# Two kinds of gate columns transposed by one product per block of tokens, the second kind at column 32 of a padded tile

## The chip, the cores and the metric

The kernel runs on one core of a Trainium2 chip. Its metric is the device time of one execution in microseconds (us), the median of several runs. A core has TensorE (PE: matrix products and transposes into PSUM), VectorE (DVE), ScalarE (ACT), GpSimd (POOL) and SyncE (SP), which here issues most of the transfers; all of them work on their own queues and wait for one another by semaphores. SBUF is the working memory of 128 partitions, and PSUM holds the results of products, in banks of 512 float32 per partition.

## The reference

One layer of a streaming encoder, for a prompt of 2048 tokens and a sample of 64 tokens with a state. A normalised and modulated input goes through one projection `w_in`, whose columns are a pooling input `u`, `q`, `k`, `v`, `o` and eight gate columns per token:

```
u, q, k, v, o, gates = jnp.split(proj, cuts, -1)
gates = gates.astype(jnp.float32) + b_gate.astype(jnp.float32)
ig = gates[..., :N_HEADS]                       # 4 input gates
lf = jax.nn.log_sigmoid(gates[..., N_HEADS:])   # 4 forget gates
...
b = jnp.cumsum(lf, -1)
dmat = b[..., :, None] - b[..., None, :] + ig[..., None, :]
```

The gates drive a matrix memory with four heads, computed in chunks. Its output and the pooling output go through `w_out`, then a gated feed-forward part with a causal convolution of width 3, and a last normalisation. All values are float32.

## The kernel before

The tokens are worked on in four attention groups of 512 tokens, the last of which has the 64 sample tokens as well (576 in all), and after all four in three feed-forward groups of 704 tokens. Activations lie transposed (features on partitions, tokens along the free dimension), and weights are streamed from HBM: SP loads them, ScalarE copies a rounded high part (line 366), VectorE subtracts it to get a low part (line 369), and each product is made of three passes over these parts. From group 1 on most attention weights come back already split (`hl_kept`, loaded by line 355).

In each attention group, `proj_v` makes the values and the gate columns first: here the activations `h` are the stationary operand, so the result has tokens on partitions, in up to five blocks (four of 128 tokens, in the last group one more of 64). The half `hv` = 1 of the weights has 264 columns: 256 of `v` and the eight gate columns. `out` copies those eight to the tile `gt` on VectorE (line 1094) and the `v` columns to `va` on ScalarE (line 1095), from the same PSUM tile. `gate_rows` then turns the gate columns into rows of tokens on four partitions (lines 1117 and 1118 transpose, 1120 adds the bias of the input gates on ScalarE, 1121 that of the forget gates on VectorE), and goes on with the log-sigmoid (lines 1125 to 1132), two scans along the tokens (1135, 1143), differences of these (1147 to 1163), a transpose back (1172) and the small tiles CL and GL that the heads use. Four heads follow (`proj_qko` with products at line 423, `lstm` at lines 1218 to 1299), then pooling and the output projection.

`gate_rows` and most other side work are generators in lists (`bg`); the loops over products call `tick`, which lets the first generator of a list run to its next `yield`, so their pieces are spread among the large products. Among the side work are the modulation sums on VectorE (`ada`, lines 201 and 203, weights loaded by line 188) and weight sums for the feed-forward part (`up_sums`, lines 843 to 868).

For the start of group 0, with its `proj_v`, and for the whole feed-forward part, the order on PE, ACT, DVE and POOL is the order of the program text (`manual_schedule`). For the rest of the attention part, and for SP's transfers throughout, a planner orders each queue by program order and its own estimate of when things are ready; it also places the tiles in memory and sets the semaphores. Small PSUM tiles are taken in turn from two pools of two banks each:

```
turn = {"mm": [large] * 4, "m2": [small, small, third, third]}
```

`m2_ps()` gives the next of the "m2" banks, `mm_ps()` one of the four large ones. `sm` is an SBUF pool with two buffers for a tile such as `gt`; the pools `a1` and `a2`, with the tiles of the attention part, are laid out behind it. `ident` is the 128 x 128 identity, and `RV` holds the two gate biases as columns.

Of the kernel before, what the change touches and what calls it, by code (L numbers as in the profile page):

```python
# [9 lines left out]
F32 = mybir.dt.float32  # L10
F32R = mybir.dt.float32r
AF = mybir.ActivationFunctionType
# [4 lines left out]
P = 128  # L17
# [42 lines left out]
def tile_layer(ctx: ExitStack, tc: tile.TileContext, xT, vecs, cst, rst, rowv, w_mod, w_ada, w_qkou, w_v, w_pool,  # L60
               w_out, w_up, w_down, st_C, st_pool, yT, o_pool, o_C, o_m, o_conv):
    nc = tc.nc
    act, dve, pool, pe = nc.scalar, nc.vector, nc.gpsimd, nc.tensor
# [9 lines left out]
    def bank(nm, shape=(P, 512)):  # L73
        q = turn[nm]
        q.append(q.pop(0))
        return q[-1].tile(list(shape), F32, tag="bank", name=nm)
# [3 lines left out]
    def mm_ps():  # L80
        return bank("mm")

    def m2_ps():
        return bank("m2")
# [7 lines left out]
    sm = actx.enter_context(tc.tile_pool(name="sm", bufs=2))  # L92

    def scr():
        return sp.tile([P, TMAX], F32, tag="scr", name="scr")
# [4 lines left out]
    def tick(i=0):  # L100
        q = bg[i]
        while q:
            try:
                next(q[0])
                return
            except StopIteration:
                q.pop(0)
# [25 lines left out]
    ident = cp.tile([P, P], F32, tag="ident", name="ident")  # L133
    nc.sync.dma_start(out=ident, in_=cst[:, C_ID:C_ID + P])
    RV = cp.tile([4, 3], F32, tag="RV", name="RV")
# [197 lines left out]
    class Unit:  # L333

        state = 0
        w = raw = None
# [494 lines left out]
    if True:  # L831
# [237 lines left out]
        def proj_v(o, h, cols):  # L1069
            nt = len(o.chunks)  # L1070
            va = a1.tile([P, 5, NH, 129], F32, tag="va", name="va")
            pool.memset(va[:, :, :, 128:129], 1.0)
            gt = sm.tile([P, 5, 8], F32, tag="gt", name="gt")

            def part(hv, kh, tis, ps, W):
                cols = VC[hv]
                for ti in tis:
                    lo, n, s = o.chunks[ti]
                    for k4 in range(4):
                        U = W.at(k4 // 2)  # L1080
                        for pi, (a, b) in enumerate(PASSES):
                            pe.matmul(ps[ti][:n, :cols], h[4 * kh + k4][:, b, lo:lo + n],  # L1082
                                      U[:, a, k4 % 2 * cols:(k4 % 2 + 1) * cols],
                                      start=(kh == 0 and k4 == 0 and pi == 0),
                                      stop=(kh == 1 and k4 == 3 and pi == 2))
                    if hv == 1 or ti % 2:
                        tick(0)
                tick(1)

            def out(hv, tis, ps):  # L1090
                for ti in tis:
                    n = o.chunks[ti][1]
                    if hv == 1:
                        dve.tensor_copy(gt[:n, ti, :], ps[ti][:n, 256:264])
                    act.activation(va[:n, ti, 2 * hv:2 * hv + 2, 0:128],
                                   ps[ti][:n, :256].rearrange("p (h v) -> p h v", v=128), AF.Copy)

            for hv in (1, 0):
                if o.g == 0:
                    out(hv, range(4), ps_v[1 - hv])  # L1100
                else:
                    ps = [mm_ps() if ti < 4 else m2_ps() for ti in range(nt)]
                    for kh in range(2):
                        part(hv, kh, range(nt), ps, Row())
                    out(hv, range(nt), ps)
                if hv == 1:
                    bg[0].append(gate_rows(o, gt, cols))
            return va

        def gate_rows(o, gt, cols):  # L1110
            T = o.T
            ir, z = scr(), scr()
            for (a, b, n, s) in o.tsegs:
                pi_, pf_ = m2_ps(), m2_ps()
                for ti in range(a, b):
                    c0 = (ti - a) * n
                    pe.transpose(pi_[:4, c0:c0 + n], gt[:n, ti, 0:4], ident[:n, :n])
                    pe.transpose(pf_[:4, c0:c0 + n], gt[:n, ti, 4:8], ident[:n, :n])
                w = (b - a) * n
                act.activation(ir[:4, a * P:a * P + w], pi_[:4, :w], AF.Identity, bias=RV[:, 0:1])  # L1120
                dve.tensor_scalar(out=z[:4, a * P:a * P + w], in0=pf_[:4, :w], scalar1=RV[:, 1:2], scalar2=None,
                                  op0=ALU.add)
            yield
            e = scr()
            dve.scalar_tensor_tensor(out=e[:4, :T], in0=z[:4, :T], scalar=-1.0, in1=z[:4, :T],
                                     op0=ALU.mult, op1=ALU.max)
            act.activation(e[:4, :T], e[:4, :T], AF.Exp, scale=-1.0)
            yield
            act.activation(e[:4, :T], e[:4, :T], AF.Ln, bias=1.0)
            yield  # L1130
            lf = z
            dve.scalar_tensor_tensor(out=lf[:4, :T], in0=z[:4, :T], scalar=0.0, in1=e[:4, :T],
                                     op0=ALU.min, op1=ALU.subtract)
            b_ = scr()
            dve.tensor_tensor_scan(out=b_[:4, :T], data0=RST[:, :T], data1=lf[:4, :T], initial=0.0,
                                   op0=ALU.mult, op1=ALU.add)
            mo = [1, GT + 2]
            for (a, b, s) in o.segs:
                w = b - a
                m0 = mo[s]  # L1140
                if s == 0 and o.g > 0:
                    dve.tensor_copy(M[:, 0:1], M[:, GT:GT + 1])
                dve.tensor_tensor_scan(out=M[:, m0:m0 + w], data0=lf[:4, a:b], data1=ir[:4, a:b],
                                       initial=M[:, m0 - 1:m0], op0=ALU.add, op1=ALU.max)
            yield
            cc = e
            dve.tensor_tensor(out=cc[:4, :T], in0=ir[:4, :T], in1=b_[:4, :T], op=ALU.subtract)
            act.activation(R4[0:4, :T], cc[:4, :T], AF.Copy)
            r = ir
            for (a, b, n, s) in o.tsegs:  # L1150
                lo, w, m0 = a * P, (b - a) * n, mo[s]
                dve.tensor_tensor(out=r[:4, lo:lo + w], in0=b_[:4, lo:lo + w], in1=M[:, m0:m0 + w], op=ALU.subtract)
                act.activation(R4[64:68, lo:lo + w], M[:, m0:m0 + w], AF.Copy, scale=-2.0)

                def v3(ap):
                    return ap.rearrange("p (t c) -> p t c", c=n)
                mp = v3(M[:, m0 - 1:m0 - 1 + w])[:, :, 0:1].broadcast_to([4, b - a, n])
                dve.tensor_tensor(out=v3(R4[32:36, lo:lo + w]), in0=v3(r[:4, lo:lo + w]), in1=mp, op=ALU.add)
                rl = v3(r[:4, lo:lo + w])[:, :, n - 1:n].broadcast_to([4, b - a, n])
                dve.tensor_tensor(out=v3(R4[96:100, lo:lo + w]), in0=v3(cc[:4, lo:lo + w]), in1=rl, op=ALU.add)  # L1160
            yield
            act.activation(RHL[0:4, :T], r[:4, :T], AF.Copy)
            dve.tensor_tensor(out=RHL[32:36, :T], in0=r[:4, :T], in1=RHL[0:4, :T].bitcast(F32), op=ALU.subtract)
            for _ in range(8):
                yield

            CL = sm.tile([P, 5, 4, 4], F32, tag="CL", name="CL")
            GL = sm.tile([P, 20], F32, tag="GL", name="GL")
            for (a, b, n, s) in o.tsegs:
                pt = m2_ps()  # L1170
                for ti in range(a, b):
                    pe.transpose(pt[:n, (ti - a) * P:(ti - a + 1) * P], R4[:, ti * P:ti * P + n], ident)
                for qn in range(4):
                    src = pt[:n, :(b - a) * P].rearrange("p (t c) -> p t c", c=P)[:, :, 32 * qn:32 * qn + 4]
                    if qn == 0:
                        dve.tensor_copy(CL[:n, a:b, qn, :], src)
                    else:
                        act.activation(CL[:n, a:b, qn, :], src, AF.Exp)
            for _ in range(4):
                yield  # L1180
            pb = m2_ps()
            for (a, b, n, s) in o.tsegs:
                sel = C[:n, (C_L127 if s == 0 else C_L63):][:, :P]
                pe.matmul(pb[:, 4 * a:4 * b], sel, CL[:n, a:b, 1, :], start=True, stop=True)
            dve.tensor_copy(GL[:, :4 * len(o.chunks)], pb[:, :4 * len(o.chunks)])
            cols += [CL, GL]
            yield
# [179 lines left out]
        for o in groups:  # L1367
# [45 lines left out]
            for gi in U_ORDER:  # L1413
                ps = proj(o, h)
                pg = poolmix(o, gi, ps, mix[gi])
# [301 lines left out]
    for o in fgroups:  # L1717
        Bo = B[o.g]
        for pi, (f0, f1_) in enumerate(PARTS):
# [82 lines left out]
            for secs in [(c,) for c in ENDS] if ends else (both,):  # L1802
                sums = [(ssum, 0)]
                for n in range(NE, KD):
                    ps = [mm_ps() for _ in secs]
# [92 lines left out]
```

## Time and profile before

| what | value |
|---|---|
| median of three runs | 2223.43 us (2221.27 to 2223.73) |
| the profiled execution, its own time | 2221.81 us |
| its span, first to last instruction | 2220.0 us |
| mean granted clock of TensorE | 0.997 |
| transpose of input-gate columns, line 1117 | 17 products |
| transpose of forget-gate columns, line 1118 | 17 products |
| copy into `gt`, line 1094 | 17 instructions |
| gate transposes at, groups 0 to 3 | 53.5, 228.6, 411.8 and 603.0 us |

Times within the profile are microseconds from the start of its span, or nanoseconds for single instructions where said. In the rows below, `m<-ident,gt 128*4 128x128` is a product that writes a small PSUM tile, with a stationary operand of 128 rows and 4 columns and a moving one of 128 x 128; `x17` is a count; in brackets stands the idle time of the engine before the instruction and what ended it. LDWEIGHTS (PEld) is the load of the stationary operand, which can overlap with products that are under way. The chain of waits follows the end of the execution back through what released each step; a duration there is the part of the instruction that lies on the chain.

### The profile page before, as it was taken

To read this page: it belongs to the slowest core of one execution; us is meant where nothing else is said; L and a number is where in the kernel's file an instruction comes from. 1 tells how busy PE (TensorE), PEld (TensorE's weight loads), DVE (VectorE), ACT (ScalarE), POOL (GpSimd) and SP (SyncE) were. 2 spreads that over 40 slices of the span, in tenths; PEclk is the share of its full clock that TensorE was granted. 3 is DMA by queue.
4 is the path that set the end of the run, shared out by engine and by line. 5 is a ranking of instruction groups with operands and counts; after the bars stand their busy time and mean duration, and the time that the engine had idled before them with its cause. 6 is when DMAs were issued, how large, how long until landed. Compare 5 with 4: busy or idle time off the path is not lost.

```text
span 2220.0 us, 38121 instructions
## 1 busy us (share of the span) xinstructions
PE 2193.5 (99%) x13798; PEld 2079.9 (94%) x13798; DVE 1567.5 (71%) x2901; ACT 1005.1 (45%) x1992; POOL 200.5 (9%) x480
## 2 busy tenths in 40 slices
PE   8999999999999999999999999999999999999998
PEld 7888888888899999999999999999999999999998
DVE  5877659577765768687858677677767685757474
ACT  3553334234343446464636444545445353445254
POOL 0010000001000101010000210000001210101012
PEclk9999999999999999999999999999999999999999
DMA  9968987997898685657656865556458554353442
GB/s 364 331 240 269 337 275 237 319 315 244 289 321 272 215 304 183 224 168 262 209 175 219 280 228 199 185 193 203 152 163 281 187 196 158 110 180 120 145 152 81
DMA packets 279358, 498.58 MB, mean 225 GB/s; under 512 B 25177, under 2 KB 105433, under 8 KB 279169
## 3 DMA queue, kind: packets, MB, share of 16 engines
q1 hardware_dynamic: 267392, 468.05, 63.3%
q10 hardware_dynamic: 11776, 28.09, 3.4%
q8 instruction: 109, 1.79, 0.3%
q14 instruction: 81, 0.66, 0.1%
HBM read 385.29 MB, written 110.75 MB: 223 GB/s over the span
## 4 chain that ended last, share of the span: by engine, by line
PE 91%; DMA 3%; DVE 3%; ACT 1%; issue 1%; SPq 0%; POOL 0%; POOLq 0%; ACTq 0%; DVEq 0%
PE mm L1487 37%; PE mm L423 24%; PE mm L1749 21%; PE mm L1082 3%; DMA wt<-wsum 1%; PE m L1263 1%; PE m L1264 1%; PE mm L1013 1%; PE m L1241 1%; PE m L1252 1%; PE m L1344 1%; PE p L1013 0%; PE m L1231 0%; PE m L1294 0%; DVE wt L369 0%
## 5 line engine op out<-in xcount | busy, mean ns | idle before, releaser
L1487 PE MATMUL mm<-hx,wt 128*128 128x352 f32 x5544 | 885.9, 321 | 4.2 <-DVE ea L1539 2.6
L1487 PEld LDWEIGHTS mm<-hx,wt 128*128 128x128 f32 x5544 | 879.1, 188 | 6.5 <-ACT wt L366 3.9
L1749 PE MATMUL mm<-av,wt 128*128 128x352 f32 (+2 forms) x3168 | 509.3, 321 | 0.5 <-DVE av L1610 0.3
L1749 PEld LDWEIGHTS mm<-av,wt 128*128 128x128 f32 x3168 | 502.6, 188 | 3.4 <-DVE av L1610 0.9
L423 PE MATMUL mm<-hl,wt 128*128 128x512 f32 (+2 forms) x1920 | 397.4, 358 | 3.9 <-DMA wt<-hl_kept 2.7
L369 DVE TENSOR_TENSOR wt<-raw,wt 128x512 fp32r<-128x512 f32 (+3 forms) x494 | 306.9, 637 | 90.6 <-ACT wt L366 85.8
L366 ACT ACTIVATE wt<-raw 128x512 fp32r<-128x512 f32 (+3 forms) x494 | 271.8, 570 | 212.7 <-PE mm L1749 83.5
L423 PEld LDWEIGHTS mm<-hl,wt 128*128 128x128 f32 x1920 | 312.3, 188 | 52.5 <-issue 6.5
L1764 DVE SCALAR_TENSOR_TENSOR x<-mm,MOD,x 128x352 f32<-128x352 f32 (+4 forms) x224 | 106.5, 526 | 115.5 <-PE mm L1749 115.4
L423 PE MATMUL mm<-mx,wt 128*128 128x512 f32 (+1 forms) x960 | 186.6, 353 | 0.0
L423 PEld LDWEIGHTS mm<-mx,wt 128*128 128x128 f32 x960 | 158.7, 188 | 25.2 <-ACT mx L1346 1.2
L1475 DVE SCALAR_TENSOR_TENSOR tg<-eg,V,tg 128x704 f32<-128x704 f32 (+1 forms) x132 | 125.7, 952 | 50.6 <-ACT tg L1470 48.3
L369 DVE TENSOR_TENSOR wt<-wt 128x512 fp32r<-128x512 f32 x176 | 121.9, 693 | 52.1 <-ACT wt L366 51.8
L366 ACT ACTIVATE wt<-wt 128x512 fp32r<-128x512 f32 x176 | 110.1, 626 | 81.4 <-DMA wt<-wsum 70.9
L1475 DVE SCALAR_TENSOR_TENSOR ta<-ea,V,ta 128x704 f32<-128x704 f32 (+1 forms) x132 | 125.6, 952 | 8.3 <-ACT ta L1470 5.9
L1610 DVE TENSOR_TENSOR av<-tg,av 128x704 fp32r<-128x704 f32 (+4 forms) x112 | 62.1, 588 | 45.1 <-ACT av L1602 44.8
L1581 ACT ACTIVATE tg<-tg 128x704 f32<-128x704 f32 (+1 forms) x66 | 52.4, 794 | 81.6 <-DVE tg L1475 76.0
L1535 ACT ACTIVATE u<-mm 128x352 f32<-128x352 f32 x66 | 30.5, 462 | 121.5 <-PE mm L1487 84.0
L1495 DVE TENSOR_TENSOR eg<-mm,u 128x352 f32<-128x352 f32 x154 | 70.1, 467 | 20.8 <-ACT u L1550 11.1
L203 DVE SCALAR_TENSOR_TENSOR acc<-raw,CA,acc 128x512 f32<-128x512 f32 x84 | 60.4, 744 | 31.7 <-DMA raw<-w_ada 31.7
L1082 PE MATMUL mm<-wt,hl 128*128 128x256 f32 (+1 forms) x576 | 70.9, 282 | 0.0
L1082 PEld LDWEIGHTS mm<-wt,hl 128*128 128x128 f32 x576 | 69.2, 188 | 1.0 <-issue 0.6
(293 smaller groups left out, 1950.9 us busy)
## 6 DMA issues: line engine op xcount, KB each, us to landing
wt<-hl_kept SPq DMA_DIRECT2D x108, 512.0 KB, 5.8
raw<-w_up SPq DMA_DIRECT2D x198, 256.0 KB, 3.8
wt<-wsum SPq DMA_DIRECT2D x176, 256.0 KB, 4.2
wt<-wsplit SPq DMA_DIRECT2D x88, 512.0 KB, 4.1
raw<-w_down SPq DMA_DIRECT2D x96, 256.0 KB, 2.8
w<-w_up SPq DMA_DIRECT2D x88, 256.0 KB, 5.7
wsum<-w SPq DMA_DIRECT2D x44, 512.0 KB, 6.4
wsplit<-wt SPq DMA_DIRECT2D x44, 512.0 KB, 4.6
```

The source lines that it names most:

```text
L203: dve.scalar_tensor_tensor(out=acc[s], in0=w, scalar=CA[:, k, s:s + 1], in1=acc[s], op0=ALU.mult, op1=ALU.add)
L366: act.activation(u.w[:, 0, :u.n], u.raw[:, :u.n], AF.Copy)
L369: dve.tensor_tensor(out=u.w[:, 1, :u.n], in0=u.raw[:, :u.n], in1=u.w[:, 0, :u.n].bitcast(F32), op=ALU.subtract)
L423: pe.matmul(ps[bi][:, :hi - lo], U[:, a, k % 4 * P:(k % 4 + 1) * P], mv[k][:, b, lo:hi], start=(at == 0 and pi == 0), stop=(k == order[-1] ...
L1082: pe.matmul(ps[ti][:n, :cols], h[4 * kh + k4][:, b, lo:lo + n], U[:, a, k4 % 2 * cols:(k4 % 2 + 1) * cols], start=(kh == 0 and k4 == 0 and ...
L1475: dve.scalar_tensor_tensor(out=t[:, :E], in0=ext[:, j:j + E], scalar=wc(j, f), in1=t[:, :E], op0=ALU.mult, op1=ALU.add)
L1487: pe.matmul(ps[:, :FH], U[:, a, kc * P:(kc + 1) * P], Bo.at(nm, kc, b), start=(first and kc == 0 and pi == 0), stop=(kc == 3 and pi == 2), ...
L1495: dve.tensor_tensor(out=ext[:, d:d + b - a], in0=ps[:, a:b], in1=u[:, a:b], op=ALU.add)
L1581: act.activation(self.tg[:, :E], self.tg[:, :E], AF.Silu)
L1610: dve.tensor_tensor(out=cut(1), in0=self.of_tg(cut(0), a, b), in1=cut(0).bitcast(F32), op=ALU.subtract)
L1749: pe.matmul(ps[i][:, :hi - lo], U[:, a, k % 4 * P:(k % 4 + 1) * P], av[k](b, lo, hi), start=(k == 0 and (a, b) == PASSES[0]), stop=(k == n ...
L1764: dve.scalar_tensor_tensor(out=x3[n][:, a:b], in0=ps[i][:, a - lo:b - lo], scalar=gt2(n, s), in1=x3[n][:, a:b], op0=ALU.mult, op1=ALU.add)
```

## The change

The tile `gt` grows from 8 to 36 columns per block and is cleared on GpSimd. The four input-gate columns stay at columns 0 to 3, the four forget-gate columns go to columns 32 to 35. One transpose of 36 columns for each block takes the place of two of 4 columns, into one PSUM tile `pg` in the place of `pi_` and `pf_`; ScalarE reads its rows 0 to 3 and VectorE its rows 32 to 35.

```
-            gt = sm.tile([P, 5, 8], F32, tag="gt", name="gt")
+            gt = sm.tile([P, 5, 36], F32, tag="gt", name="gt")
+            pool.memset(gt, 0.0)
...
                     if hv == 1:
-                        dve.tensor_copy(gt[:n, ti, :], ps[ti][:n, 256:264])
+                        dve.tensor_copy(gt[:n, ti, :].rearrange("p (a b) -> p a b", b=4)[:, 0:9:8, :],
+                                        ps[ti][:n, 256:264].rearrange("p (a b) -> p a b", b=4))
...
             for (a, b, n, s) in o.tsegs:
-                pi_, pf_ = m2_ps(), m2_ps()
+                pg = m2_ps()
                 for ti in range(a, b):
                     c0 = (ti - a) * n
-                    pe.transpose(pi_[:4, c0:c0 + n], gt[:n, ti, 0:4], ident[:n, :n])
-                    pe.transpose(pf_[:4, c0:c0 + n], gt[:n, ti, 4:8], ident[:n, :n])
+                    pe.transpose(pg[:36, c0:c0 + n], gt[:n, ti, :], ident[:n, :n])
                 w = (b - a) * n
-                act.activation(ir[:4, a * P:a * P + w], pi_[:4, :w], AF.Identity, bias=RV[:, 0:1])
-                dve.tensor_scalar(out=z[:4, a * P:a * P + w], in0=pf_[:4, :w], scalar1=RV[:, 1:2], scalar2=None,
+                act.activation(ir[:4, a * P:a * P + w], pg[:4, :w], AF.Identity, bias=RV[:, 0:1])
+                dve.tensor_scalar(out=z[:4, a * P:a * P + w], in0=pg[32:36, :w], scalar1=RV[:, 1:2], scalar2=None,
                                   op0=ALU.add)
```

## The prediction

> **What bounds the kernel now.** I read the page first, for the engine that fills the span and the chain that ended last.
>
> ```profile
> span 2220.0 us, 38121 instructions
> PE 2193.5 (99%) x13798; PEld 2079.9 (94%) x13798; DVE 1567.5 (71%) x2901; ACT 1005.1 (45%) x1992; POOL 200.5 (9%) x480
> PE 91%; DMA 3%; DVE 3%; ACT 1%; issue 1%; SPq 0%; POOL 0%; POOLq 0%; ACTq 0%; DVEq 0%
> ```
>
> TensorE is busy for 2193.5 of 2220.0 us and carries 91% of the chain, so a product taken off its queue is worth its place in that queue, as long as no other engine or transfer is late next. The change works on the gate columns, so the second view was that of the two lines that transpose them.
>
> ```profile
> L1117 PEld LDWEIGHTS m<-ident,gt x17: 78/84/85, 53.2 to 604.0; 128*4 128x4 f32 x16, 64*4 64x4 f32 x1
> L1117 PE MATMUL m<-ident,gt x17: 214/272/273, 53.5 to 604.0; 128*4 128x128 f32 x16, 64*4 64x64 f32 x1
> L1118 PE MATMUL m<-ident,gt x17: 215/273/273, 53.6 to 604.1; 128*4 128x128 f32 x16, 64*4 64x64 f32 x1
> ```
>
> There are 34 of them: 16 blocks of 128 tokens and one of 64, twice. Their 272 ns are durations, not places in the queue. For the places I took the timeline of TensorE in group 1 and the chain of waits in group 3:
>
> ```profile
> 228.57 0.27 PE L1117 MATMUL m<-ident,gt 128*4 128x128 f32 x1
> 228.68 0.27 PE L1118 MATMUL m<-ident,gt 128*4 128x128 f32 x1
> ...
> 229.33 0.27 PE L1118 MATMUL m<-ident,gt 128*4 128x128 f32 x1
> ...
> 604.07 0.14 PE m L1117
> 604.21 0.06 PE m L1118
> ```
>
> From 228.57 to 229.33 seven steps pass, 0.109 us each. The 64-token product costs 0.06 us on the chain. Third, who stops TensorE in the attention stage, and how full the transfers are around the gate work (the columns are busy times of PE, PEld, DVE, ACT and POOL, then granted clock, DMA share, GB/s):
>
> ```profile
> PE mm L423 <- DMA wt<-hl_kept: 2.7, 2, 2.4
> PE m L1263 <- DVE st L1257: 1.7, 1, 1.7
> PE mm L423 <- DVE wt L369: 0.8, 1, 0.8
> PE mm L423 <- ACT wt L366: 0.5, 1, 0.5
> 225.00:290.00 65.00, 65.00 (x384) 55.18 (x383) 43.85 (x98) 23.76 (x63) 2.54 (x3) 1.00 0.97 330
> 405.00:470.00 65.00, 62.33 (x371) 52.33 (x370) 44.10 (x90) 21.22 (x50) 2.46 (x2) 0.97 0.91 310
> 600.00:690.00 90.00, 88.28 (x676) 83.42 (x674) 57.87 (x144) 36.31 (x105) 4.20 (x5) 1.00 0.93 311
> ```
>
> After the gate transposes of group 1 TensorE never stops (65.00 of 65.00 us); in group 2 it loses 2.67 us and in group 3 1.72 us, with the DMA engines at 0.91 to 0.97. In those stretches time saved on TensorE can be lost to a transfer.
>
> **The change part by part: products removed.** The seventeen products of L1118 go: 16 x 0.109 + 0.06 = 1.80 us of TensorE's queue, 0.44 us in each of groups 0 to 2 and 0.50 us in group 3. The seventeen that stay load 36 columns in place of 4. Bounds for that are transposes of full 128-column tiles:
>
> ```profile
> L1172 PEld LDWEIGHTS m<-ident,R x17: 110/141/143, 70.4 to 628.0; 128*128 128x128 f32 x16, 128*64 128x64 f32 x1
> 70.75 0.44 PE m L1172 x4
> 95.44 0.59 PE m L1231 x4
> ```
>
> Even with 128 columns, whose load takes 141 ns where 4 take 84, a transpose holds the chain for 0.44 / 4 = 0.110 us, at worst 0.148 (L1231). A load of 36 columns lies between, nearer to 4, and is hidden under the product before it: I take 0, with a bound of 17 x (0.148 - 0.109) = 0.66 us. By the Trainium skill, "TensorE: Matmul & The Clock Gate", section "LDWEIGHTS (loading the stationary operand)", a load costs its columns over 1.2, in ns, which speaks against the padding: 32 more columns are an estimated 27 ns for each of the 17, 0.45 us that the sum would lose if loads were not hidden. The trace doesn't bear it out in that form, since 124 more columns cost 57 ns of load and about 1 ns of pitch.
>
> **Products removed: what is late next.** Group 0's order is written by hand and its chain runs through the gates:
>
> ```profile
> 54.43 0.68 ACT L1120 ACTIVATE scr<-m,RV 4x512 f32<-4x512 f32 x1 [1.01 <-PE m L1117]
> 54.54 0.74 DVE L1121 TENSOR_SCALAR scr<-m,RV 4x512 f32<-4x512 f32 x1 [2.59 <-PE m L1118]
> 55.12 1.28 ACT L1127 ACT_TABLE_LOAD   x1
> 55.31 0.68 DVE L1125 SCALAR_TENSOR_TENSOR scr<-scr 4x512 f32<-4x512 f32 x1
> 56.42 0.63 ACT L1127 ACTIVATE scr<-scr 4x512 f32<-4x512 f32 x1
> ...
> 62.05 0.65 DVE L1147 TENSOR_TENSOR scr<-scr 4x512 f32<-4x512 f32 x1
> 62.64 0.67 DVE L369 TENSOR_TENSOR wt<-raw,wt 128x512 fp32r<-128x512 f32 x1
> 63.36 2.80 PE L423 MATMUL mm<-hl,wt 128*128 128x512 f32 x11 [0.77 <-DVE wt L369]
> ```
>
> TensorE waits here at 63.36 us for VectorE, which is behind the gate arithmetic. So group 0 gains not its 0.44 us, but what the gate chain gains. ScalarE starts when the last of the i-transposes is done, three products earlier than now: 54.43 - 0.33 = 54.10. VectorE must now read the tile that ScalarE reads. A row of the waits shows that these two are put one behind the other when they read one PSUM tile:
>
> ```profile
> ACT va L1095 <- DVE gt L1094: 33.6, 13, 9.6
> ```
>
> So I count this as an added wait: z (L1121) starts at 54.10 + 0.68 + 0.02 = 54.80 and not at 54.54, and L1125 ends at 54.80 + 0.74 + 0.03 + 0.68 = 56.25. The exponential needs that and its table (54.79 + 1.28 = 56.07), so it starts at about 56.30 in place of 56.42. Group 0 gains 0.12 us; without the added wait, the table's end decides and it gains 0.33. Queued behind z on VectorE are L1125 and the low parts of the weights (L369), and on these TensorE waits. By the Trainium skill, "PSUM — Partial Sum Buffer", section "PSUM bank collisions raise a hardware error", two engines must be kept apart only on one bank and one quadrant of 32 partitions; rows 0 to 3 and 32 to 35 are different quadrants, so by that rule no wait would be needed, and the sum would be 0.21 us better. No run here shows such a pair yet.
>
> In group 2 the first stop of any size after the transposes is a transfer:
>
> ```profile
> 432.88 0.67 DVE acc L203
> 433.55 0.14 SPq L188
> ...
> 433.79 7.19 DMA wt<-hl_kept
> ...
> 441.12 0.94 PE mm L423 x3
> ```
>
> The weights that TensorE waits for 2.42 us were issued behind VectorE's modulation sums, which wait for transfers themselves; the gate step is not what held them. I take group 2's 0.44 us as lost in this wait (bound: all of it kept). Group 1 has no stop behind it and keeps 0.44. In group 3 the transfers ahead of the stop at 676.8 us follow TensorE's own progress, so I let it keep 0.50.
>
> **The two engines and GpSimd.** The copies into the padded tile have the same 8 values in two runs of 4; the row bounds a change at a few ns, and ScalarE's copy behind each is not on the chain. The clearing of the padded tile is new, 128 x 180 values, four times:
>
> ```profile
> L1072 POOL MEMSET va<- x4: 133/134/134, 14.2 to 519.2; 128x20 f32 x4
> L1052 POOL MEMSET R<- 128x576 f32 x1 | 0.6, 577 | 0.0
> L1094 DVE COPY gt<-mm x16: 154/164/167, 49.6 to 600.7; 128x8 f32<-128x8 f32 x16
> ```
>
> It lies between 0.13 and 0.58 us, about 0.25. It follows the clearing of va, which is at 14.2 us for a copy at 49.6, and at 519.2 for one near 600. GpSimd is 9% busy. The cover is some 35 us at the least: nothing. Without that cover it would cost its 0.25 us per group.
>
> **Placement.** The padded tile is 720 bytes per partition and not 160, in two buffers, so the tiles that are laid out after it move by 1.1 KB or so. The rows show the like only as the two pitches of a transpose, 0.110 and 0.148; 68 transposes at L1231 between these are 68 x 0.038 = 2.6 us either way. Nothing in the profile ties the pitch to an address, so I take 0.
>
> **Sum.** 0.12 + 0.44 + 0 + 0.50 = 1.06 us, bounds 0 and 1.80. The profiled execution took 2221.81 us, 1.81 over its span and 1.62 under the median of 2223.43. So it would become about 2220.7, and the median 2222.4: 0.05% faster. About 0.2%, or 4.4 us, can be told from no change.
>
> **The rivals.** *A, the planner's order gets worse: slower.* In groups 1 to 3 the order of each queue comes from a planner that starts from its own estimate of times; the change moves z behind ScalarE, takes products out and moves a bank of PSUM on for all later small tiles. Place: VectorE in front of the sums of L203. Their reads free the buffers for the next w_ada loads, and behind these on SP stands wt<-hl_kept, as at 433.55 us. Price: a load of weights one place later costs the measured 2.4 us. It decides from the point where the new waits exceed 4.4 + 1.06 = 5.5 us, that is from three of them. One in each of the three stretches gives 2222.4 + 7.2 = 2229.6. For it: DMA shares of 0.91 to 0.97 leave no room to catch up. Against it: in group 1 TensorE doesn't stop even at 0.97, and VectorE has idle time where z stands (before L1121 in group 0, 2.59 us).
>
> *B, the order gets better: faster.* If the new order happens to remove the two stops of groups 2 and 3 as well, the gain is 2.7 + 1.7 + 1.80 = 6.2 us: 2217.2. For it: both stops are small accidents of order between transfers. Against it: it needs both, and nothing in the change aims at them.
>
> *C, a transpose is worth its duration: faster.* At 272 ns each, the seventeen would be 17 x 0.272 = 4.6 us: 2218.8. The Trainium skill, "TensorE: Matmul & The Clock Gate", "Part 4: PE-mode transpose", gives about 275 ns in one kernel's context, as the duration row here has it. The steps of 0.109 us between starts speak against it.
>
> *D, no gain left: no change.* The wider load and the stops take all of it: 2223.4.
>
> **How the numbers follow.** My forecast of 2222.4 gets 0.42 and D 0.08, both within 0.2%: 0.50. A gets 0.30, since the scheduled stretches are full of transfers and a chance order has more ways to cost than to gain. B gets 0.17 and C 0.03: 0.20 for faster. The range goes down to 2216.5, just past B, and up to 2230.0, just past A's three waits; about 0.05 is left below and 0.15 above. The likeliest case alone lies from 2221.6 (all 1.80 us kept) to 2223.4.
>
> **What would show it.** Right: 17 products with a 128x36 load at about 0.11 us of the queue, 17 instructions fewer for PE; in group 0 ScalarE's first gate step earlier by 0.3 us against TensorE, and VectorE's z directly behind ScalarE's end; waits of TensorE between 110 and 760 us close to 4.4 us in all. A would show as further rows "PE mm L423 <- DMA wt<-hl_kept" or stops on VectorE in those stretches, B as both rows gone. If the difference lies in the feed-forward stage, behind 800 us, or in the pitch of products that the change doesn't touch, the prediction is wrong in its reasons whatever the time.

## The result

| what | before | after |
|---|---|---|
| median of 12 runs each, alternating | 2223.31 us (2220.58 to 2226.88) | 2226.64 us (2224.34 to 2231.53) |
| ratio, 95% interval | | 1.0021 [1.0014, 1.0029] |
| profiled execution, its own time | 2221.81 us | 2228.43 us |
| longest stop of TensorE in group 0 behind the gates | 0.77 us | 2.84 us |
| mean granted clock | 0.997 | 0.995 |

The change makes the kernel slower, by 0.21%, about 4.7 us (3.1 to 6.4); the ratio is taken over all the runs, and the two medians by themselves lie 3.3 us apart. The change does what it says: the page of the changed kernel has 17 products fewer, and the load of 36 columns takes 98 ns.

```profile
span 2226.6 us, 38087 instructions
PE 2198.3 (99%) x13781; PEld 2080.3 (93%) x13781; DVE 1567.9 (70%) x2901; ACT 1003.9 (45%) x1992; POOL 202.6 (9%) x484
PE 92%; DMA 2%; DVE 2%; ACT 1%; issue 1%; POOL 0%; SPq 0%; ACTq 0%; POOLq 0%; DVEq 0%
```

```profile
L1119 PEld LDWEIGHTS m<-ident,gt x17: 93/98/99, 54.9 to 611.3; 128*36 128x36 f32 x16, 64*36 64x36 f32 x1
L1119 PE MATMUL m<-ident,gt x17: 229/272/273, 55.1 to 611.3; 128*36 128x128 f32 x16, 64*36 64x64 f32 x1
```

TensorE is busy 4.8 us longer with fewer products. So the same products must have run slower somewhere, and the place is found by laying the starts of the same large products beside each other, after minus before (products into `mm` with 256 moving columns or more, by their count in the trace):

| product number | 96 | 108 | 132 | 156 | 720 | 840 | 1440 | 1620 | 2160 | 2340 | end |
|---|---|---|---|---|---|---|---|---|---|---|---|
| us later | 1.64 | 1.23 | 1.55 | 6.32 | 7.21 | 6.60 | 6.78 | 6.41 | 7.64 | 7.22 | 6.62 |

Numbers 96 to 108 enclose the gate transposes of group 0. The loss, 4.77 us, comes between 132 and 156, just behind them. The next three pairs (720 and 840, 1440 and 1620, 2160 and 2340) enclose the gate transposes of groups 1 to 3, and each gains. The 1.64 us ahead of the gates arise where both kernels do the same; in the profiles of the runs below, the delay that a kernel brings from its first 33 us lay between -0.8 and +2.2.

Here are ScalarE and VectorE in the changed kernel's timeline for that place (start, busy time, engine, line, operation; in brackets the idle time before it and what ended it):

```profile
55.74 0.68 ACT L1121 ACTIVATE scr<-m,RV 4x512 f32<-4x512 f32 x1 [0.83 <-PE m L1119]
56.46 0.74 DVE L1122 TENSOR_SCALAR scr<-m,RV 4x512 f32<-4x512 f32 x1 [3.16 <-ACT scr L1121]
...
57.95 0.63 ACT L1128 ACTIVATE scr<-scr 4x512 f32<-4x512 f32 x1 [0.22 <-DVE scr L1126]
...
59.88 0.60 ACT L1192 ACTIVATE q<-mm 128x512 f32<-128x512 f32 x1 [1.30 <-PE mm L423]
60.49 1.28 ACT L1130 ACT_TABLE_LOAD   x1
...
61.79 0.63 ACT L1130 ACTIVATE scr<-scr 4x512 f32<-4x512 f32 x1
62.72 0.63 ACT L366 ACTIVATE wt<-raw 128x512 fp32r<-128x512 f32 x1 [0.30 <-DMA raw<-w_qkou]
...
65.65 0.63 ACT L1154 ACTIVATE R<-M 4x512 f32<-4x512 f32 x1 [2.30 <-DVE M L1144]
66.30 0.63 ACT L366 ACTIVATE wt<-raw 128x512 fp32r<-128x512 f32 x1
```

And ScalarE in the kernel before:

```profile
57.07 1.28 ACT L1129 ACT_TABLE_LOAD   x1
58.36 0.63 ACT L1129 ACTIVATE scr<-scr 4x512 f32<-4x512 f32 x1
58.90 0.57 ACT L1191 ACTIVATE q<-mm 128x512 f32<-128x512 f32 x1
61.17 0.63 ACT L366 ACTIVATE wt<-raw 128x512 fp32r<-128x512 f32 x1 [1.70 <-DMA raw<-w_qkou]
62.22 0.63 ACT L1153 ACTIVATE R<-M 4x512 f32<-4x512 f32 x1 [0.42 <-DVE M L1143]
```

Before, ScalarE loads the table and takes the logarithm (L1129), and then copies q (L1191). After, the copy of q (L1192) stands ahead of the logarithm (L1130): ScalarE waits 1.30 us for TensorE's q product, and only then loads the table and takes the logarithm, which starts at 61.79 in place of 58.36 (1.23 us of that is the delay that this execution has at product 108). The scans follow it on VectorE. ScalarE's copy of the scan (L1154) now waits 2.30 us, and the high part of the next weights (L366, 66.30) is queued behind that copy. These are TensorE's rows for the same 31 products, the first from the changed kernel's timeline, the second from that of the kernel before:

```profile
66.98 10.09 PE L423 MATMUL mm<-hl,wt 128*128 128x512 f32 x31 [2.84 <-ACT wt L366]
```

```profile
63.36 7.38 PE L423 MATMUL mm<-hl,wt 128*128 128x512 f32 x31 [0.77 <-DVE wt L369]
```

TensorE stops 2.84 us, and then its 31 products take 10.09 us where the same 31 took 7.38 before. The windows say why (PE, PEld, DVE, ACT and POOL busy, then granted clock, DMA share, GB/s), first after:

```profile
67.00:70.00 3.00, 3.00 (x7) 2.42 (x8) 2.90 (x5) 2.01 (x4) 0.00 (x0) 0.50 1.05 406
70.00:73.00 3.00, 3.00 (x8) 2.29 (x8) 2.97 (x8) 0.91 (x2) 0.00 (x0) 0.52 1.05 407
73.00:76.00 3.00, 3.00 (x15) 2.45 (x14) 3.00 (x5) 0.97 (x1) 0.00 (x0) 1.00 1.06 403
```

then before:

```profile
67.00:70.00 3.00, 3.00 (x15) 2.46 (x14) 3.00 (x7) 1.37 (x2) 0.00 (x0) 1.00 1.05 391
```

For some six microseconds behind the stop the granted clock is about one half, and TensorE makes 7 or 8 products in three microseconds in place of 15. PE shows as busy all that time. The sum for the place: stops 0.81 + 2.84 after against 0.49 + 0.77 before, 2.39 us; slower products 10.09 - 7.38 = 2.71 us; together 5.10, beside the measured 5.09 between products 108 and 156 (6.32 - 1.23). The first of the two stops lies ahead of product 132, so 4.77 us come behind it.

So the theory to be tested: z has to wait for ScalarE on the shared PSUM tile; the planner, which counts this, orders ScalarE's queue in group 0 in another way; a stop of over two microseconds follows, and it costs as much again in clock. The rivals: the padded, moved and cleared tile costs the time by itself; or fewer products, by moving everything after them, change the order.

### The profile page after: what moved, and what is told of

The parts are those of the page before. It is cut to its first block, busy times and chain, and to the rows that moved or that the text cites. A ratio compares the mean times of both kernels' runs of the same rounds, so it can differ in the third digit from the quotient of the medians.

```text
span 2226.6 us, 38087 instructions
## 1 busy us (share of the span) xinstructions
PE 2198.3 (99%) x13781; PEld 2080.3 (93%) x13781; DVE 1567.9 (70%) x2901; ACT 1003.9 (45%) x1992; POOL 202.6 (9%) x484
## 3 DMA queue, kind: packets, MB, share of 16 engines
q8 instruction: 109, 1.79, 0.3%
## 4 chain that ended last, share of the span: by engine, by line
PE 92%; DMA 2%; DVE 2%; ACT 1%; issue 1%; POOL 0%; SPq 0%; ACTq 0%; POOLq 0%; DVEq 0%
PE mm L1488 37%; PE mm L423 24%; PE mm L1750 21%; PE mm L1083 3%; DMA raw<-w_down 1%; PE m L1253 1%; PE m L1242 1%; PE mm L1013 1%; PE m L1264 1%; PE m L1265 1%; PE m L1345 1%; PE p L1013 0%; PE m L1232 0%; PE m L1295 0%; DVE wt L369 0%
## 5 line engine op out<-in xcount | busy, mean ns | idle before, releaser
L369 DVE TENSOR_TENSOR wt<-raw,wt 128x512 fp32r<-128x512 f32 (+3 forms) x494 | 307.0, 637 | 92.0 <-ACT wt L366 86.2
L366 ACT ACTIVATE wt<-raw 128x512 fp32r<-128x512 f32 (+3 forms) x494 | 271.5, 570 | 213.0 <-PE mm L1750 91.2
L369 DVE TENSOR_TENSOR wt<-wt 128x512 fp32r<-128x512 f32 x176 | 121.7, 692 | 47.2 <-ACT wt L366 47.1
L366 ACT ACTIVATE wt<-wt 128x512 fp32r<-128x512 f32 x176 | 110.0, 625 | 68.6 <-DMA wt<-wsum 60.7
```

Of the source, the lines that this page charges most:

```text
L366: act.activation(u.w[:, 0, :u.n], u.raw[:, :u.n], AF.Copy)
L369: dve.tensor_tensor(out=u.w[:, 1, :u.n], in0=u.raw[:, :u.n], in1=u.w[:, 0, :u.n].bitcast(F32), op=ALU.subtract)
```

## The experiments

Ratios are to the kernel before, run alternately on the same chip, with 95% intervals. Unless said otherwise, each ran three to five rounds.

**The change again.** No edit.

> The changed kernel once more, for a second profile. Theory T1 (in group 0 the planner put the copy of q ahead of the logarithm on ScalarE; the gate chain comes late, the weights behind it too, TensorE stands for 2.84 us at 66.98 and then runs at half clock for some 5 us): the same stop and the same clock of about 0.50 behind it, 2226 to 2227 us. Rival T2 (the cost lies in the tiles that moved in memory, the clearing on GpSimd or the wider product): the stop varies, the time stays. The 1.6 us that the profile lost before 50 us, where the order of the queues is that of before, should be gone or smaller if it is chance, and be there again if moved tiles cause it.

Measured: 2230.21 us, 1.0028 [1.0018, 1.0038]. Stops of 1.20 and 2.45 us in the same places, and the clock again at one half behind the second:

```profile
66.67 10.14 PE L423 MATMUL mm<-hl,wt 128*128 128x512 f32 x31 [2.45 <-ACT wt L366]
```

```profile
67.00:70.00 3.00, 3.00 (x8) 2.35 (x8) 2.88 (x6) 1.69 (x4) 0.00 (x0) 0.50 1.06 408
```

The median lies 3 us above what was expected; the stop, the clock and the place come again, so they aren't those of one execution. This profile too begins late, by 1.35 us.

**The change with the logarithm ahead of q, as before.** All of the change stays; one line of order is added for group 0.

```
-            evac(o, proj(o, h), q, AF.Copy)
+            ps = proj(o, h)
+            if o.g == 0 and not hasattr(o, "q_out"):
+                o.q_out = True
+                with tc.issue_after(o.ln.ins):
+                    evac(o, ps, q, AF.Copy)
```

> The changed kernel with one constraint: in group 0 the copy of q on ScalarE is queued behind the logarithm, as it stands before the change. T1: the gate chain comes some 1.3 to 1.9 us earlier, the stop at 67 us falls from 2.84 to under 1 us, the clock stays at 1.00 behind it: 2.84 - 0.8 + 3.0 = 5 us less, 2221 to 2223 us. T2: 2226 to 2227 us, no change.

Measured: 2223.64 us, 1.0002 [0.9994, 1.0011]: the loss is gone. ScalarE and TensorE in its timeline, and the window behind the stop:

```profile
60.52 0.63 ACT L1130 ACTIVATE scr<-scr 4x512 f32<-4x512 f32 x1
61.06 0.57 ACT L1192 ACTIVATE q<-mm 128x512 f32<-128x512 f32 x1
```

```profile
65.53 7.41 PE L423 MATMUL mm<-hl,wt 128*128 128x512 f32 x31 [1.26 <-DVE wt L369]
```

```profile
67.00:70.00 3.00, 3.00 (x14) 2.39 (x13) 2.91 (x5) 2.06 (x4) 0.00 (x0) 1.00 1.05 405
```

The start of the logarithm is 1.27 us earlier than in the changed kernel although ScalarE's gate step began 0.64 us later in this execution (56.38 against 55.74). The stop is 1.26 us, where under 1 us was expected, and the 31 products take 7.41 us: the clock holds. With its shared tile, padding and clearing untouched, the change is no longer slower, so the order of group 0 carries the loss.

**The change with z written ahead of ScalarE's gate step.** The two readers of the shared tile change places in the text, so that VectorE reads first and ScalarE waits.

```
-                act.activation(ir[:4, a * P:a * P + w], pg[:4, :w], AF.Identity, bias=RV[:, 0:1])
                 dve.tensor_scalar(out=z[:4, a * P:a * P + w], in0=pg[32:36, :w], ...)
+                act.activation(ir[:4, a * P:a * P + w], pg[:4, :w], AF.Identity, bias=RV[:, 0:1])
```

> The changed kernel with z (VectorE) written ahead of the input-gate rows (ScalarE), so that ScalarE waits for VectorE on the shared PSUM tile and not the other way. The planner then leaves the logarithm ahead of q by itself. T1: stop at 67 us under 1.5 us, clock kept, 2221 to 2224 us, perhaps 0.5 us above the run with the constraint since the exponential starts later. T2: 2226 to 2227 us.

Measured: 2226.93 us, 1.0022 [1.0013, 1.0030], not what was expected: the shared tile costs as much with its readers in this order. The logarithm did come first, but the planner now put ScalarE's copy of the scan ahead of the next weights:

```profile
60.16 0.63 ACT L1130 ACTIVATE scr<-scr 4x512 f32<-4x512 f32 x1
...
64.01 0.63 ACT L1154 ACTIVATE R<-M 4x512 f32<-4x512 f32 x1 [2.75 <-DVE M L1144]
64.67 0.63 ACT L366 ACTIVATE wt<-raw 128x512 fp32r<-128x512 f32 x1
```

```profile
65.35 2.88 PE L423 MATMUL mm<-hl,wt 128*128 128x512 f32 x8 [3.05 <-ACT wt L366]
```

So it is not only "q ahead of the logarithm": what stops TensorE is weights queued on ScalarE behind a copy that waits for the scan. The place of q matters because it makes the scan late.

**The kernel before, with q ahead of the logarithm.** None of the change, only the new order of these two.

```
+            if o.g == 0 and not hasattr(o, "q_out"):
+                o.q_out = True
+                tc.add_manual_dep(o.ln.ins, o.qev.ins.name, ...)   # order only, no semaphore
```

> The kernel before, with nothing of the change but the order: in group 0 the logarithm on ScalarE is queued behind the copy of q. T1: the gate chain is 1.3 us late, TensorE stops for 2 to 3 us around 65 us and its clock halves for some us: 2226 to 2229 us. T2: the order costs nothing, 2223 to 2224 us.

Measured: 2224.28 us, 1.0007 [0.9998, 1.0015]: less than expected. The stop grew from 0.77 to 1.96 us and the clock fell, but for a shorter time:

```profile
65.55 3.65 PE L423 MATMUL mm<-hl,wt 128*128 128x512 f32 x9 [1.96 <-DVE wt L369]
```

```profile
65.00:68.00 3.00, 2.45 (x7) 1.96 (x8) 2.97 (x6) 2.38 (x5) 0.00 (x0) 0.71 1.06 395
68.00:70.00 2.00, 2.00 (x6) 1.53 (x6) 1.95 (x3) 0.88 (x3) 0.00 (x0) 0.59 1.06 394
```

Against the kernel before this execution loses 2.75 us between products 120 and 156. Its total, though, is not resolved from no change. This order by itself brings the stop. In the changed kernel the stop is longer; there it ends on the weights' high part, which stands behind the copy of the scan, and here on a low part (L369).

**The kernel before with the padded tile.** The padding, the clearing and the copy in two runs, but two transposes of 4 columns into two PSUM tiles.

```
-            gt = sm.tile([P, 5, 8], F32, tag="gt", name="gt")
+            gt = sm.tile([P, 5, 36], F32, tag="gt", name="gt")
+            pool.memset(gt, 0.0)
...
-                    pe.transpose(pf_[:4, c0:c0 + n], gt[:n, ti, 4:8], ident[:n, :n])
+                    pe.transpose(pf_[:4, c0:c0 + n], gt[:n, ti, 32:36], ident[:n, :n])
```

> The kernel before with the padded tile, its clearing on GpSimd and the copy in two runs, but still two transposes of 4 columns into two PSUM tiles (columns 0 to 3 and 32 to 35). The order of all queues is that of before. T1 (the order in group 0 costs the time): as before, 2223 to 2224 us. T2 (moved tiles, clearing or copies cost it): as the changed kernel, 2226 to 2227 us.

Measured: 2224.14 us, 1.0005 [0.9996, 1.0014]. The order in group 0 is that of before, its two stops are 0.99 and 0.28 us, and nothing is lost there (1.42 us behind the kernel before at product 120, 1.44 at 156). The padding and clearing aren't what the change loses.

**The change with the stop filled.** 22 products without use (the identity by itself, into the gate tile after its readers) are put into TensorE's queue where the long stop was.

```
+                if o.g == 0 and at == 4 and pi == 1:
+                    o.turns = getattr(o, "turns", 0) + 1
+                    if o.turns == 2:
+                        for _ in range(22):
+                            tc.keep_in_program_order(pe.matmul(o.pg[:, 0:P], ident, ident, ...))
```

> The changed kernel with 22 products of 128 x 128 (about 0.11 us each, 2.4 us in all) that nobody reads, put on TensorE ahead of the product of k at which it stands for 2.84 us at 66.98 us. The weights come no earlier, so the stop is only filled. If half of the loss is the granted clock that falls after a stop of over 2 us: the clock stays at 1.00 from 64 to 76 us and the time falls by about 3 us, to 2223 to 2224.5 us. If the stop alone counts, or the clock falls for another reason: 2226 to 2227.5 us.

Measured: 2227.14 us, 1.0022 [1.0012, 1.0033]. The old stop was filled and the clock stayed at 1.00 there, but the planner brought a small product of the gate step forward (L1192, which makes GL from CL), and it waited 2.22 us until 78.77, and the clock fell behind this one:

```profile
76.00:79.00 3.00, 0.78 (x4) 0.34 (x3) 2.97 (x6) 0.46 (x4) 0.00 (x0) 0.96 1.06 402
79.00:82.00 3.00, 3.00 (x8) 2.02 (x8) 1.63 (x4) 0.36 (x1) 0.00 (x0) 0.50 1.05 392
```

The time says nothing on what the clock alone costs, as the order moved again. The rows say that the half clock goes with the stop, wherever that is.

**The weights first, in the change and in the kernel before.** In group 0, three constraints of order: q's copy behind the logarithm, the second scan behind the low part of one set of weights, and ScalarE's copy of the scan behind the high part of the next.

```
+            behind(o.qev, o.ln)
...
+                behind(o.scan, LO[11])
+                behind(o.rc, HI[12])
```

> The changed kernel with three constraints in group 0: q's copy behind the logarithm, the second scan on VectorE behind the low part of the weights that TensorE waits for, the copy of M on ScalarE behind the high part of the next weights. T1: TensorE waits only for the weights themselves, the stops at 62 to 67 us fall to 1 us or less, the clock is kept: 2221 to 2223 us, perhaps below before. T2: 2226 to 2227 us.

> The kernel before with the same three constraints, so that ScalarE and VectorE have the same order in group 0 as in the run with the changed kernel. The difference of these two is what the products are worth by themselves: by the sum of the prediction the changed one should be 1.0 to 1.8 us faster, which the intervals may not resolve; T2 would have it 3 us slower. This one by itself: 2222 to 2223.5 us.

Measured: the change with them 2223.22 us, 1.0001 [0.9992, 1.0010]; the kernel before with them 2222.17 us, 0.9998 [0.9989, 1.0007]. Lines are six further down in these two kernels:

```profile
63.97 6.27 PE L429 MATMUL mm<-hl,wt 128*128 128x512 f32 x25 [0.86 <-ACT wt L372]
```

```profile
63.39 6.95 PE L429 MATMUL mm<-hl,wt 128*128 128x512 f32 x28 [0.98 <-ACT wt L372]
```

With one and the same order in group 0, the stops are 0.86 and 0.98 us and the change is no longer slower than the kernel before. Neither is resolvably faster than the kernel before. The change was expected to be 1.0 to 1.8 us faster of the two. Compared directly (11 runs each, on one chip, by ranks), it is 1.0 us slower, with a 95% interval from 0.8 us faster to 2.5 us slower: the 1.8 us that the removed products free are not in the total. In the two profiles they are there for a while. Counted from the start, the change gains 2.1 us on the other kernel by product 3200 (758 us), and loses 4.2 us in what follows, nearly all of it the feed-forward part, where it does nothing. These are single executions; why the gain doesn't last stays open.

**As many products as before: in one tile, and in two.** Both have 34 transposes of 36 columns. The first makes each transpose twice into the shared tile; the second makes them into two PSUM tiles, one for each reader.

```
                     pe.transpose(pg[:36, c0:c0 + n], gt[:n, ti, :], ident[:n, :n])
+                    pe.transpose(pg[:36, c0:c0 + n], gt[:n, ti, :], ident[:n, :n])
```

```
-                pg = m2_ps()
+                pg, pf_ = m2_ps(), m2_ps()
...
+                    pe.transpose(pf_[:36, c0:c0 + n], gt[:n, ti, :], ident[:n, :n])
...
-                dve.tensor_scalar(out=z[...], in0=pg[32:36, :w], ...)
+                dve.tensor_scalar(out=z[...], in0=pf_[32:36, :w], ...)
```

> The changed kernel with each transpose of 36 columns done twice into the same PSUM tile, so 34 products as before, and one tile that both engines read. T1a (what makes the planner put q first is that VectorE's z has to wait behind ScalarE on the shared tile): q stands ahead of the logarithm, TensorE stops for over 2 us between 62 and 68 us and its clock falls: 2226 to 2229 us. T1b (it is the time that the removed products free on TensorE): the logarithm is first, 2223 to 2224.5 us.

> The same 34 products of 36 columns, but into two PSUM tiles: ScalarE reads rows 0 to 3 of the one, VectorE rows 32 to 35 of the other, so that neither waits for the other. T1a: logarithm first, no stop over 2 us, clock kept, 2223 to 2224.5 us. T1b: the same. T2 (the wide product, the padded tile or the clearing costs the time): 2226 to 2228 us.

Measured: one tile 2225.55 us, 1.0012 [1.0004, 1.0021]; two tiles 2224.16 us, 1.0008 [1.0000, 1.0016]. One tile, with z behind ScalarE and q at 60.41 ahead of the logarithm:

```profile
57.01 0.74 DVE L1123 TENSOR_SCALAR scr<-m,RV 4x512 f32<-4x512 f32 x1 [3.96 <-ACT scr L1122]
60.41 0.60 ACT L1193 ACTIVATE q<-mm 128x512 f32<-128x512 f32 x1 [1.29 <-PE mm L423]
66.73 3.49 PE L423 MATMUL mm<-hl,wt 128*128 128x512 f32 x14 [1.67 <-DVE wt L369]
```

Two tiles, with z 0.11 us behind ScalarE's start and the logarithm ahead of q:

```profile
55.71 0.68 ACT L1122 ACTIVATE scr<-m,RV 4x512 f32<-4x512 f32 x1 [1.16 <-PE m L1119]
55.82 0.74 DVE L1123 TENSOR_SCALAR scr<-m,RV 4x512 f32<-4x512 f32 x1 [2.79 <-PE m L1120]
59.65 0.63 ACT L1131 ACTIVATE scr<-scr 4x512 f32<-4x512 f32 x1
60.19 0.57 ACT L1193 ACTIVATE q<-mm 128x512 f32<-128x512 f32 x1
64.66 5.58 PE L423 MATMUL mm<-hl,wt 128*128 128x512 f32 x23 [0.30 <-DVE wt L369]
```

With the number of products the same, the planner puts q first only where the tile is shared. So the shared PSUM tile turns the order, and not the number of products. The expected stop of over 2 us did not come: the one-tile kernel's stop of 1.67 us left the clock at 1.00, and it loses 1.14 us between products 120 and 156, not 4 to 5. The price of this order depends on how long its stop becomes, and on where it falls (last section). That the two times differ isn't resolved.

**The moved tiles alone, and cleared.** The kernel before with `gt` allocated 36 columns wide and only its first 8 in use; in the second run also cleared.

```
-            gt = sm.tile([P, 5, 8], F32, tag="gt", name="gt")
+            gt = sm.tile([P, 5, 36], F32, tag="gt", name="gt")[:, :, 0:8]
+            pool.memset(gt, 0.0)                    # second run only
```

> The kernel before with the gate tile allocated 36 columns wide and only 8 used, not cleared: the tiles laid out behind it move as in the changed kernel, and the order of all queues and all instructions stay. Of the nine profiles with the wide tile, eight lost 0.9 to 2.2 us against the first profile of before by 30 us; of three without it, one did (1.06 us). If the moved tiles cause that: about 1.3 us by 30 us again, and 2223.5 to 2224.5 us. If it is chance or the clearing: anything from -0.8 to 1.1 us by 30 us, and as before within 0.05%.

> The same with the clearing on GpSimd as well (128 x 180 values at about 14.3 us, 0.25 us). If the clearing delays the start: 1.3 us by 30 us here and none in the run without it. If the moved tiles do: the same in both. If neither: both like before.

Measured: 2224.59 us, 1.0008 [0.9998, 1.0018], and 2223.34 us, 1.0003 [0.9993, 1.0013], with the order of before in both. By 30 us they were 0.9 and 0.8 us behind the profile of before, where 1.3 was forecast for both if the moved tiles made the start late. No cost of place or clearing is shown. All the kernels with a wide tile and the old order came out between 1.0003 and 1.0008, though, and a cost of up to 0.1% from the moved addresses isn't excluded by these runs.

## Why the prediction was wrong

**What bounds the kernel: right, with one row misread.** TensorE's queue does bound it. But the row of 405 to 470 us quoted in the prediction shows a granted clock of 0.97 beside a stop, and the prediction read only the 2.67 us of idle time from it. 0.03 x 65 is about another 2 us, lost behind that stop (1.7 by the windows in the last section, 0.27 x 2.90 + 0.31 x 3.00). The price of a stop was there to be seen.

**Products removed: right.** From the start of the product ahead of the gate transposes to the start of the one behind them, TensorE takes 0.59, 0.47, 0.47 and 0.81 us in groups 0 to 3, where it took 1.03, 0.91, 0.91 and 1.28: 1.79 us less, where the prediction had 1.80. The 36-column load takes 98 ns and starts keep their 0.109 us. The offsets of the table fall by 0.41, 0.61, 0.37 and 0.42 us, and that these too come to 1.81 is luck. Group 1's 0.61 holds something that the prediction had not: behind the transposes the 256-column products start 0.113 us apart and not 0.118, in all eight profiles with a load of 36 columns and in none of the six with 4. In group 2 the stop on `wt<-hl_kept` is still there (2.44 us) and takes the gain, as forecast: 0.37 us had been gained by product 1620, well ahead of it, but nothing of that is left at product 1800, behind it, which is 7.62 us late against 6.78 at product 1440. In group 3 the stop of 1.7 us at L1263 is gone, half of what rival B needed. It is gone in all six profiles of kernels with 17 gate transposes and there, at 0.8 to 2.2 us, in all eight with 34. So the sum put at nothing a gain that the change does bring.

**The added wait: right in its size, to a hundredth.** z starts directly behind ScalarE (55.74 + 0.68 = 56.42, z at 56.46). The exponential starts at 57.95; less the 1.64 us by which this execution is later, that is 56.31, forecast 56.30. By the Trainium skill, "PSUM — Partial Sum Buffer", section "PSUM bank collisions raise a hardware error", rows 0 to 3 and 32 to 35 need no such wait. The trace has it all the same: it is one of the program's semaphores, and no run had the two readers on one tile without it.

**"Group 0's order is written by hand": the step that failed.** In group 0 only the start, up to `proj_v`, is under `manual_schedule`. `gate_rows`, q, k and the weights that follow stand in the planner's order, from the very place at which the gates begin. The prediction therefore let ScalarE's and VectorE's order in group 0 stand and moved it by 0.12 us, a gain; measured from product 108 to 156, group 0 loses 5.09 us. In its place the runs show: the shared tile makes the planner put q ahead of the logarithm (one tile against two), this order brings the stop (the change with the logarithm first, and the kernel before with q first), and the stop carries the loss.

**Clearing and copies: right.** The clearing takes 0.25 us on GpSimd, 246 to 248 ns in each group, and no wait of TensorE ends on it. **Placement: not settled**, as above.

**Rival A** had the mechanism's kind, an order of the planner that gets worse through z behind ScalarE, but the wrong place and price. It looked on VectorE in groups 1 to 3, and needed three stops of 2.4 us. It was one stop, on ScalarE in group 0, which cost 2.39 us of waiting and 2.71 us of clock. Between 110 and 760 us, where A would have shown, the waits became fewer: 4.4 us before, 2.6 after. **B** came about by half and was outweighed; **C** is excluded by the 1.79 us; **D** is excluded by the interval.

The measured 2226.64 us lies within the range, and the forecast of a small gain lies outside the interval on the other side. What stays open: where the 1.8 us of freed queue goes in the total once the order is repaired (the change with the logarithm first lies at 1.0002, that with the weights first at 1.0001, and their intervals are 0.0017 and 0.0018 wide), and whether the moved tiles take any of it. That the start varies by a microsecond or two between profiles goes with the clock. Between 13 and 26 us it did not fall at all in two of the 14 profiles (0.3 and 0.8 us ahead of the kernel before), fell for 3.41 us in four (that of the kernel before, and three that are 0.7 to 1.2 behind it), and for two or three times as long in eight (0.8 to 2.2 behind), around a stop of 2.1 us that all 14 have there.

## What to carry to other kernels

Before the order of a stretch is taken as fixed, find in the code where the hand-written part ends: behind it, an added wait is also an input to the planner; here z came 0.6 us later behind ScalarE's start (0.72 against 0.11), and the new order cost eight times that. Two readers of one PSUM tile are a dependence between two engines, so a product saved by sharing a tile has to be weighed against that chain. Price a stop of TensorE by its idle time and by the granted clock of the windows behind it, and look at stops that already exist for the second figure.

## What the hardware showed unexpectedly

A stop of about two microseconds can make TensorE slow after it as well. Behind the gates of group 0 the longest stops of 0.77, 1.26 and 1.67 us left the granted clock at 1.00; those of 1.96, 2.45, 2.84 and 3.05 us, and the 2.22 us one of the filled kernel, brought it to between 0.50 and 0.71 in a window behind them. In group 2 the wait for `wt<-hl_kept` shows the same in kernels that the order of group 0 doesn't concern. Windows of the kernel before, behind its stop of 2.42 us at 441.12:

```profile
436.00:439.00 3.00, 2.70 (x13) 1.91 (x11) 1.92 (x3) 0.27 (x1) 0.00 (x0) 1.00 1.04 359
...
441.10:444.00 2.90, 2.88 (x9) 1.76 (x10) 1.04 (x2) 0.34 (x2) 0.00 (x0) 0.73 0.97 330
444.00:447.00 3.00, 3.00 (x18) 2.87 (x17) 2.60 (x5) 0.81 (x4) 0.00 (x0) 0.69 1.07 400
```

The length of the stop alone doesn't decide. In the change with the logarithm first, a stop of 2.06 us in the feed-forward part left the clock at 1.00, and in the kernel before with the padded tile one of 1.64 us, with 0.34 us more right behind it, brought it down; the stop, and a window behind it, of the one and of the other:

```profile
925.96 9.27 PE L1494 MATMUL mm<-hx,wt 128*128 128x352 f32 x57 [2.06 <-DVE ea L1546]
```

```profile
926.00:929.00 3.00, 3.00 (x19) 3.00 (x20) 1.81 (x4) 1.30 (x3) 0.00 (x0) 1.00 0.55 188
```

```profile
1358.14 0.59 PE L1751 MATMUL mm<-av,wt 128*128 128x352 f32 x2 [1.64 <-ACT av L1604]
```

```profile
1360.00:1363.00 3.00, 3.00 (x13) 3.00 (x13) 2.68 (x6) 1.51 (x3) 0.00 (x0) 0.54 0.42 122
```

The records of the clock in the 14 traces show where it turns. Within one profile the falls begin whole multiples of 3.413 us apart (those of the kernel before at 19.18, 442.43 and 2213.95 us, 124 and 643 steps from the first). Each fall but the one that runs into the end of the kernel lasts one, two or three such steps, at a clock of one half, so that one step costs an estimated 3.413 x 0.5 = 1.7 us at most. Counted by these steps between 26 and 2190 us, a step at full clock in which TensorE stood for 1.88 us or more in all was always followed by a fall, one with up to 1.56 us never, and between these it went either way. So a stop is dear if most of it falls into one step: the stop of 2.06 us lies 0.50 in one and 1.56 in the next. By the Trainium skill, "TensorE: Matmul & The Clock Gate", "Part 1: The HAM clock gate", the clock halves after an idle window of about 3.4 us. These traces show the half clock and steps of that length, but standing for about half of a step was enough.
